# The passage from the z products into the SSD: a hand order on three engines, z's PSUM buffers swapped, two chunks prepared between z tiles

## The chip, the cores and the metric

One core of one Trainium2 chip. The metric is the device time of one execution, in microseconds (us). The engines are TensorE (PE, with PEld for its weight loads), VectorE (DVE), ScalarE (ACT), GpSimd (POOL) and SyncE (SP, which issues DMAs).

## The reference

One layer of an encoder over 1024 positions of width 1024: adaptive normalisation, one input projection, a Mamba-2 SSD group beside a chunked attention group, an output projection, then a gated convolutional FFN and a last normalisation. The part that matters here:

```
z, xbc, dt_raw, q, k, v = split(h @ w_in)
dt    = softplus(dt_raw + dt_bias);   A = -exp(a_log)
y     = ssd_scan(xs * dt, dt * A, bm, cm) + d_skip * xs      # per chunk, state carried on
y_ssd = rmsnorm(y * silu(z), norm_w)
x     = x + g_m * (concat[y_ssd, y_att] @ w_out)
```

In the kernel an SSD chunk has 128 positions (8 chunks). For each chunk: a decay mask per head `exp(seg) * (C B^T)` in two groups of 4 heads; `y_diag` (mask times `xdt = x * dt`); `y_off` (C times the state before); the new state (`xdd`, x with dt and the decay to the end, times B).

## The kernel before, in words

The program is a stream of instructions written in Python. A scheduler with its own timeline chooses the order on each engine, except where the code pins it: `tc.issue_after(i)` puts an instruction behind `i`, and the proxies `V`, `A`, `T` (class `InOrder`, for VectorE, ScalarE, TensorE) keep the written order while their `on` is true. In the SSD loop the helper `pe` chains TensorE's instructions in the order written. High-precision products are three matmuls of split operands (`mm3`, lines 76 to 78): high by high, high by low, low by high; `split` (lines 80 to 86) makes the high part on ScalarE and the low part on VectorE.

The stages around the change, in order:

- **z products.** h (`hH`, `hL`) times z's weights, in two column halves of 260 (`ch` 1, then 0), each in 8 tiles of 128 rows (`st` 0 to 7), 24 matmuls of 260 columns a tile. The weights of a half come in four parts (`wz_weights`): loaded into `raws`, split into `wzh` on ScalarE and `wzl` on VectorE. A tile lands in PSUM, either in a buffer of pool `psv` (tags `acc` and `pv`, named `zps`) or in one of two `s` buffers, and is emptied by a tanh on ScalarE (`zt`, line 628) and a multiply on VectorE (`zs`, line 629).
- **dt.** `dt_prep`: softplus of the 8 dt columns (`sm_...`), `adt`, its split `adh`/`adl`, sums over the chunk by three matmuls, and their exponentials (`ex`).
- **W_out.** Eight slots, loaded into `wos` or `raws` by `wout_get`, four of them scaled by a gate row (`wout_fold`), split by `wout_split` into the space of h (`hH`, `hL`) that z no longer needs. Slots 0 to 3 multiply the attention part, 4 to 7 the SSD part.
- **Preparing a chunk** (`ssd_pre`): `xdt` on VectorE, `xdd` on GpSimd, for each group the matrix `rm` (ScalarE and VectorE), its product `sg`, the products and transposes `cb`, and the mask `th` = exp(sg) * cb.
- **SSD loop**, chunk c: `ssd_y` (products `ydp`, `yop`, `stp`; then y, its gate with `zs`, its normalisation), `ssd_turn` of the chunk before (four transposes into `xps`, copied to `xs`), `ssd_pre` of chunk c + 1, and the output projection `wout_half(c)` (`wops`, 24 matmuls, whose right operand `yhl` is the split of attention or SSD output).

[...] While z runs, `acc` and `pv` are banks 0 and 1, the two `s` buffers banks 2-3 and 4-5, `tp` 6 and 7. In the SSD loop `xps` has 0 and 1, `wops` 2 and 3, and 4 to 7 go to `ydp`, `yop`, `stp`, `sg`; chunk 0's `ydp` is bank 4. In z's second half tile 7 has bank 4 before the change.

Of the kernel before, what the change touches and what calls it, by code (L numbers as in the profile page):

```python
# [40 lines left out]
def f32(ap):  # L41
    return ap.bitcast(F32)
# [22 lines left out]
def tile_block(ctx: ExitStack, tc: tile.TileContext, x, crep, pk, w_ada, w_first, w_ft, w_z,  # L65
# [14 lines left out]
    def split(hi, lo, src, ehi, elo, scale=None):  # L80
        if scale is not None:
            A.activation(hi, src, AF.Copy, scale=scale)
            V.scalar_tensor_tensor(lo, src, scale, f32(hi), op0=ALU.mult, op1=ALU.subtract)
            return
        i = A.activation(hi, src, AF.Copy) if ehi is A else ehi.tensor_copy(hi, src)  # L85
        return i, elo.tensor_tensor(lo, src, f32(hi), ALU.subtract)  # L86
# [501 lines left out]
    def wout_split(slot, t):  # L588
        dh, j = WORDER[slot]
        h, l = (n[slot // 4][:, slot % 4].rearrange("p a b -> p (a b)") for n in (hth, htl))  # L590
        with tc.issue_after(pin[0]), tc.issue_after(pin[1]):
            if j < 2:
                split(h, l, t, A, V)
            else:
                for b in range(2):
                    c = slice(512 * b, 512 * b + 512)
                    k = SNW + order[2 * j + b]
                    split(h[:, c], l[:, c], t[:, c], A, V, scale=pkt[:, k:k + 1])
        ws[dh] += [(h[:, k:k + 512], l[:, k:k + 512]) for k in (0, 512)]

    def rm512():
# [12 lines left out]
            ws.append((th_, tl_))  # L614
        return ws

    def z_tile(ch, st, wz):
        if st % 4 < 2:
            ps = psv.tile([P, 512], F32, tag=("acc", "pv")[st % 4], bufs=1, name="zps")[:, 0:260]
        else:  # L620
            ps = s_tile()[:, 0:260]
        for kt in range(KT):
            mm3(ps, hth[st // 4][:, st % 4, kt, :], htl[st // 4][:, st % 4, kt, :],
                wz[kt // 2][0][:, kt % 2, :],
                wz[kt // 2][1][:, kt % 2, :], kt == 0, kt == KT - 1)
# [3 lines left out]
        V.scalar_tensor_tensor(zs[:, st, ch * 260:ch * 260 + nz], th[:, 0:nz], 1.0, ps[:, 0:nz],
                               op0=ALU.add, op1=ALU.mult)  # L630
        if ch == 1:
            V.scalar_tensor_tensor(zs[:, st, 512:520], ps[:, 252:260], 2.0,
                                   pkt[:, DTB:DTB + 8], op0=ALU.mult, op1=ALU.add)

    def dt_prep():
# [13 lines left out]
        V.scalar_tensor_tensor(sm["p"], sm["p"], 1.0, sm["t"], op0=ALU.add, op1=ALU.mult)  # L649
        V.tensor_scalar(c8(sm["t"]), dtr, 0.0, None, op0=ALU.max)  # L650
        V.scalar_tensor_tensor(sm["dt"], sm["p"], 2.0, sm["t"], op0=ALU.mult, op1=ALU.add)
        V.scalar_tensor_tensor(sm["adt"].rearrange("p (c h) -> p c h", c=8),
                               sm["dt"].rearrange("p (c h) -> p c h", c=8), -1.0,
                               na.unsqueeze(1).to_broadcast([P, 8, 8]), op0=ALU.mult, op1=ALU.mult)
        pin[:] = [i.ins for i in split(adh, adl, sm["adt"], A, V)]
# [13 lines left out]
    def pe(op, *a, **k):  # L669
        with tc.issue_after(chain[0]) if chain and chain[0] else ExitStack():  # L670
            i = op(*a, **k)  # L671
# [3 lines left out]
    def ssd_pre(c, xp_, sgp_, between=None):
        cs = slice(c * P, (c + 1) * P)
# [3 lines left out]
        G.tensor_tensor(h8(xdd), h8(xdt), hb("de", c), ALU.mult)  # L680
        ms_ = []
        for g in range(2):
            rm = bcp.tile([P, 2, 4, P], F32R, tag="rm", bufs=2, name="rm")
            hs = slice(c * 8 + 4 * g, c * 8 + 4 * g + 4)
            for h in range(4):
                A.activation(rm[:, 0, h, :], tle, AF.Copy, scale=f32(adh)[:, hs.start + h:hs.start + h + 1])
            if g == 0:
                V.tensor_tensor(rm[:, 1], tle.unsqueeze(1).to_broadcast([P, 4, P]),
                                f32(adl)[:, hs].unsqueeze(2).to_broadcast([P, 4, P]), ALU.mult)
            else:  # L690
                for h in range(4):
                    A.activation(rm[:, 1, h, :], tle, AF.Copy,
                                 scale=f32(adl)[:, hs.start + h:hs.start + h + 1])
            sg = sgp_()
            for i in range(2):
                pe(T.matmul, sg, sgtr, rm[:, i].rearrange("p h l -> p (h l)"), start=i == 0, stop=i == 1)
            if g == 0:
                cbp = xp_()
                for i in range(2):
                    pe(T.matmul, cbp[:, i * P:(i + 1) * P], bt_[i][:, cs], ct_[i][:, cs],  # L700
                       start=True, stop=True)
                for i in range(2):
                    pe(T.transpose, cbp[:, (2 + i) * P:(3 + i) * P], bt_[i][:, cs], ident)
                cb = bcp.tile([P, 4, P], F32, tag="cb", bufs=1, name="cb")
                V.tensor_tensor(cb.rearrange("p (a b) l -> p a b l", a=2),
                                cbp.rearrange("p (a b l) -> p a b l", a=2, b=2),
                                tle1.unsqueeze(2).to_broadcast([P, 2, 2, P]), ALU.mult)
# [30 lines left out]
            wout_fold(wt[j])  # L738
    wz = wz_weights(0)
    wout_get(5, 2)  # L740
    for st in range(NT):
        z_tile(0, st, wz)
        if st == 0:
            wout_fold(wt[5])
            dt_prep()
        if st == 3:
            for j in (0, 1, 2):
                wout_split(j, wt[j])
            wout_get(3, 6, 7)
# [734 lines left out]
```

## Time and profile before

| what | us |
|---|---|
| median of 3 runs | 1232.65 (1231.15 to 1232.92) |
| profiled execution: span from first to last instruction | 1234.8 |
| profiled execution: its own time outside the span | not given by the page |
| TensorE (PE) busy | 1169.8 (95%) |
| VectorE (DVE) busy | 944.7 (77%) |
| ScalarE (ACT) busy | 589.0 (48%) |
| GpSimd (POOL) busy | 199.9 (16%) |
| z's second half, from its first product | 408.18 in the span |
| chunk 0's first product | 440.15 |
| chunk 1's first product | 453.12 |

Times in the lists below count from the first instruction. A timeline row has the start, the duration, engine, line of the code, operation, output and inputs, shapes, how many such instructions in a row, and in brackets the idle time of the engine before it with what ended it. In a row of waits the three numbers are the sum, how often, and the longest. The granted clock is the share of TensorE's full clock. A matmul of plain fp32 shows as two records.

### The profile page before, as it was taken

The page shows a single profiled execution, that of the slowest core. Times are in us where ns is not written, and L with a number is a line of the kernel's source. Part 1 is how long each engine was busy: PE and PEld are TensorE (multiplying, and loading weights), DVE is VectorE, ACT ScalarE, POOL GpSimd, SP SyncE. Part 2 cuts the span into 40 slices and gives each one's busy share as a digit, 9 for nine tenths or more (in the row PEclk, how much of TensorE's full clock was granted, in tenths as well). Part 3 has the DMA queues.
Part 4 walks back from the last instruction along what each step waited for, and adds up shares of the span by engine and source line. Part 5 has one row for each costly group of instructions (what it writes and reads, how often), then busy time and mean ns, then how long its engine had stood idle before and what let it go on. Part 6 is the DMA issues. An engine that isn't in the chain of part 4 may idle for free.

```text
span 1234.8 us, 15648 instructions
## 1 busy us (share of the span) xinstructions
PE 1169.8 (95%) x5802; PEld 983.1 (80%) x5802; DVE 944.7 (77%) x1419; ACT 589.0 (48%) x991; POOL 199.9 (16%) x174
## 2 busy tenths in 40 slices
PE   4998999989999969999999999999999999999995
PEld 3787788878878958888778888888888888888884
DVE  6836545589689667746799989888889869766976
ACT  4525555573333556666554434453434435433443
POOL 1304555575120033400000000000000000000002
PEclk9999999999999989999999999999999999999998
DMA  8712112134355301123132333222332277733533
GB/s 332 254 36 80 48 44 68 54 115 154 120 180 197 121 1 43 44 94 111 37 117 92 113 128 119 86 77 103 128 128 77 95 281 257 279 120 127 171 120 136
DMA packets 56395, 150.86 MB, mean 122 GB/s; under 512 B 5632, under 2 KB 5760, under 8 KB 54912
## 3 DMA queue, kind: packets, MB, share of 16 engines
q1 hardware_dynamic: 49264, 125.49, 29.8%
q10 hardware_dynamic: 7056, 24.38, 4.9%
q8 instruction: 45, 0.74, 0.2%
q14 instruction: 30, 0.25, 0.1%
HBM read 116.56 MB, written 29.10 MB: 118 GB/s over the span
## 4 chain that ended last, share of the span: by engine, by line
PE 80%; DVE 11%; ACT 3%; DMA 2%; issue 2%; POOL 1%; SPq 0%; DVEq 0%; POOLq 0%; ACTq 0%
PE wops L671 6%; PE dn L77 6%; PE dn L76 6%; PE dn L78 6%; PE uY L76 5%; PE uY L78 5%; PE uY L77 5%; PE uZ L78 3%; PE uZ L76 3%; PE uZ L77 3%; PE uX L76 3%; PE uX L78 3%; PE uX L77 3%; PE acc L76 2%; PE acc L77 2%; PE acc L78 2%
## 5 line engine op out<-in xcount | busy, mean ns | idle before, releaser
L903 POOL TENSOR_TENSOR st<-st,mhalf 128x1 f32<-128x1 f32 x16 | 12.7, 798 | 691.9 <-DVE st L902 680.5
L76 PE MATMUL dn<-w 128*128 128x512 f32 x308 | 111.9, 389 | 0.0
L77 PE MATMUL dn<-w 128*128 128x512 f32 x308 | 111.9, 389 | 0.0
L395 POOL TENSOR_SCALAR p<-p,st 128x640 f32<-128x640 f32 (+4 forms) x64 | 99.0, 1561 | 26.8 <-DVE st L394 23.7
L78 PE MATMUL dn<-w 128*128 128x512 f32 x308 | 103.3, 389 | 0.0
L76 PE MATMUL uY<-tH,w 128*128 128x512 f32 x256 | 99.7, 389 | 1.8 <-ACT w L58 1.8
L77 PE MATMUL uY<-tL,w 128*128 128x512 f32 x256 | 99.6, 389 | 0.0
L78 PE MATMUL uY<-tH,w 128*128 128x512 f32 x256 | 99.6, 389 | 0.0
L85 ACT ACTIVATE w<-ya 128x1024 fp32r<-128x1024 f32 (+1 forms) x41 | 39.1, 954 | 85.0 <-PE uY L78 82.7
L671 PE MATMUL wops<-hH,yhl 128*128 128x512 f32 x224 | 74.8, 402 | 3.5 <-DVE yhl L86 2.1
L76 PEld LDWEIGHTS dn<-w 128*128 128x128 f32 x308 | 57.8, 188 | 12.1
L77 PEld LDWEIGHTS dn<-w 128*128 128x128 f32 x308 | 57.8, 188 | 12.0
L78 PEld LDWEIGHTS dn<-w 128*128 128x128 f32 x308 | 57.8, 188 | 11.9
L389 DVE CUSTOM_DVE_ANT_0 p<-s,bias 128x640 f32<-128x640 f32 (+4 forms) x64 | 40.7, 650 | 26.3 <-PE tp L421 8.7
L76 PEld LDWEIGHTS uY<-tH,w 128*128 128x128 f32 x256 | 48.0, 188 | 12.0 <-ACT w L58 2.2
L78 PEld LDWEIGHTS uY<-tH,w 128*128 128x128 f32 x256 | 48.1, 188 | 10.0
L77 PEld LDWEIGHTS uY<-tL,w 128*128 128x128 f32 x256 | 48.0, 188 | 10.0
L86 DVE TENSOR_TENSOR pt<-tp,pt 128x512 fp32r<-128x512 f32 (+2 forms) x72 | 41.6, 595 | 18.4 <-ACT pt L85 11.4
L85 ACT ACTIVATE w<-xs 128x1024 fp32r<-128x1024 f32 (+1 forms) x41 | 38.9, 952 | 32.3 <-PE uY L78 32.3
L671 PEld LDWEIGHTS wops<-hH,yhl 128*128 128x128 f32 x224 | 42.4, 190 | 12.9 <-DVE yhl L86 2.5
L76 PE MATMUL s<-hH,wh 128*128 128x512 f32 x128 | 50.5, 395 | 1.5 <-DVE ct L492 1.3
L1054 DVE SCALAR_TENSOR_TENSOR a<-cv,pkt,a 128x1023 f32<-128x1023 f32 (+1 forms) x40 | 51.2, 1279 | 0.1
(444 smaller groups left out, 3428.8 us busy)
## 6 DMA issues: line engine op xcount, KB each, us to landing
gz<-a ACTq DMA_DIRECT2D x10, 1024.0 KB, 5.3
wos<-in_w_ada_dram SPq DMA_DIRECT2D x18, 512.0 KB, 4.1
ya<-in_w_up_dram SPq DMA_DIRECT2D x11, 768.0 KB, 4.1
xs<-in_w_up_dram SPq DMA_DIRECT2D x11, 768.0 KB, 4.2
adat<-in_w_ada_dram SPq DMA_DIRECT2D x16, 512.0 KB, 5.7
raws<-in_w_ft_dram SPq DMA_DIRECT2D x14, 512.0 KB, 3.5
qk<-in_w_ada_dram SPq DMA_DIRECT2D x14, 512.0 KB, 4.7
gy<-a ACTq DMA_DIRECT2D x10, 512.0 KB, 2.6
```

Of the source, the lines that this page charges most:

```text
L76: T.matmul(ps, lh, rh, start=start, stop=False, skip_group_check=more)
L77: T.matmul(ps, lh, rl, start=False, stop=False, skip_group_check=more)
L78: T.matmul(ps, ll, rh, start=False, stop=stop, skip_group_check=more)
L85: i = A.activation(hi, src, AF.Copy) if ehi is A else ehi.tensor_copy(hi, src)
L86: return i, elo.tensor_tensor(lo, src, f32(hi), ALU.subtract)
L389: V.tensor_tensor_reduce(out=dst, in0=src, in1=bsl, scale=-1.0, scalar=3e38, op0=ALU.add, op1=ALU.min, accum_out=nm)
L395: G.tensor_scalar(pv_, pv_, rr, None, op0=ALU.mult)
L671: i = op(*a, **k)
L903: G.tensor_tensor(r, ms, mhalf[:, 0:1], ALU.pow)
L1054: V.scalar_tensor_tensor(a[:, j:S], c[:, 0:S - j], w[2 - j], a[:, j:S], op0=ALU.mult, op1=ALU.add)
```

## The change

It changes the stretch from z's second half (`ch` 0) to the first SSD chunks:

1. z tiles use the `s` buffers for `st` 0, 1, 4, 5 and `acc`/`pv` for 2, 3, 6, 7, in both halves (before, the other way round). In the second half tile 7 now has bank 1 and tile 5 bank 4.
2. From the first z tile of half 0 on, `V`, `A` and `T` are in order, as written; TensorE's order goes on into the SSD loop's chain, VectorE's and ScalarE's ends after chunk 0's `ssd_y`.
3. `z_tile`, `dt_prep` and `ssd_pre` are cut into parts, and the parts are written between the z tiles: `dt_prep` behind tile 0, the sums (`dt_sums`) behind tile 1, chunk 0's masks behind tiles 2 to 4, chunk 1's `rm`, `xdt` and `xdd` behind tile 5, W_out's splits in between and after.
4. `wout_split` has no `issue_after` pins any more.

```diff
     def wout_split(slot, t):
...
-        with tc.issue_after(pin[0]), tc.issue_after(pin[1]):
-            if j < 2:
-                split(h, l, t, A, V)
...
+        if j < 2:
+            split(h, l, t, A, V)
...
-    def z_tile(ch, st, wz):
-        if st % 4 < 2:
-            ps = psv.tile([P, 512], F32, tag=("acc", "pv")[st % 4], bufs=1, name="zps")[:, 0:260]
+    def z_mm(ch, st, wz):
+        if st % 4 > 1:
+            ps = psv.tile([P, 512], F32, tag=("acc", "pv")[st % 4 - 2], bufs=1, name="zps")[:, 0:260]
         else:
             ps = s_tile()[:, 0:260]
...
-    for st in range(NT):
-        z_tile(0, st, wz)
-        if st == 0:
-            wout_fold(wt[5])
-            dt_prep()
-        if st == 3:
-            for j in (0, 1, 2):
-                wout_split(j, wt[j])
-            wout_get(3, 6, 7)
-            pre0 = ssd_pre(0, tp_tile, tp_tile)
-            wout_split(3, wt[3])
-        if st >= 4:
-            wout_split(st, wt[st])
+    V.on = A.on = T.on = True
+    V.last = A.last = T.last = None
+    zp = z_mm(0, 0, wz)
+    dt_prep()
+    z_evac(0, 0, zp)
+    zp = z_mm(0, 1, wz)
+    r0 = pre_rm(0, 0)
+    dt_sums()
+    x0 = pre_x(0)
+    z_evac(0, 1, zp)
+    wout_split(0, wt[0])
+    zp = z_mm(0, 2, wz)
+    r1 = pre_rm(0, 1)
+    g0 = pre_sg(r0, tp_tile())
+    z_evac(0, 2, zp)
+    zp = z_mm(0, 3, wz)
+    cb = pre_cb(0, tp_tile())
+    m0 = pre_m(0, g0, cb)
+    wout_fold(wt[5])
+    wout_split(1, wt[1])
+    z_evac(0, 3, zp)
+    zp = z_mm(0, 4, wz)
+    g1 = pre_sg(r1, tp_tile())
+    wout_split(2, wt[2])
+    wout_get(3, 6, 7)
+    m1 = pre_m(1, g1, cb)
+    pre0 = *x0, cb, [m0, m1]
+    z_evac(0, 4, zp)
+    zp = z_mm(0, 5, wz)
+    pre1 = {g: pre_rm(1, g) for g in range(2)}
+    pre1["x"] = pre_x(1)
+    z_evac(0, 5, zp)
+    zp = z_mm(0, 6, wz)
+    wout_split(3, wt[3])
+    wout_split(4, wt[4])
+    z_evac(0, 6, zp)
+    zp = z_mm(0, 7, wz)
+    wout_split(5, wt[5])
+    z_evac(0, 7, zp)
+    for j in (6, 7):
+        wout_split(j, wt[j])
...
-    chain[:] = [None]
+    T.on = False
+    chain[:] = [T.last]
     for c in range(NT):
         y = ssd_y(c, *pre)
+        V.on = A.on = False
```

What stands on the engines, with buffer numbers. In the changed kernel an instruction of a proxy that is in order has the line of `InOrder.issue` (L58).

TensorE at the start of z's second half, before (`zps_3779` is tile 0, `zps_3833` tile 1, `s_3861` tile 2; `wzh_3755` and `wzl_3756` are the first part of the weights, `wzh_3760` the second):

```order
L76 MATMUL zps_3779<-wzh_3755,hH0_83 128x260
L76 MATMUL zps_3833<-wzh_3755,hH0_83 128x260
L76 MATMUL s_3861<-wzh_3755,hH0_83 128x260
L77 MATMUL zps_3779<-wzl_3756,hH0_83 128x260
L78 MATMUL zps_3779<-wzh_3755,hL0_85 128x260
```

and now (`s_3779` is tile 0; `wzh_3765` and `wzl_3766` are the third part):

```order
L58 MATMUL s_3779<-wzh_3760,hH0_83 128x260
L58 MATMUL s_3779<-wzl_3761,hH0_83 128x260
L58 MATMUL s_3779<-wzh_3760,hL0_85 128x260
L58 MATMUL s_3779<-wzh_3765,hH0_83 128x260
L58 MATMUL s_3779<-wzl_3766,hH0_83 128x260
```

Before, tiles take turns; now the 24 matmuls of tile 0 follow each other through all four parts, and tile 1's stand behind them.

VectorE at the end of z, before (`s_4033` is tile 6, `s_4065` tile 7, `hL` W_out's low parts, `ydp_4135` chunk 0's product):

```order
L86 TENSOR_TENSOR hL0_85<-wos_2874,hH0_83 128x1024
L83 SCALAR_TENSOR_TENSOR hL1_86<-wos_2874,pkt_66,hH1_84 128x512 x2
L83 SCALAR_TENSOR_TENSOR hL1_86<-raws_68,pkt_66,hH1_84 128x512 x2
L83 SCALAR_TENSOR_TENSOR hL1_86<-wos_2874,pkt_66,hH1_84 128x512
L629 SCALAR_TENSOR_TENSOR zs_2862<-zt_4058,s_4033 128x260
L83 SCALAR_TENSOR_TENSOR hL1_86<-wos_2874,pkt_66,hH1_84 128x512
L83 SCALAR_TENSOR_TENSOR hL1_86<-raws_68,pkt_66,hH1_84 128x512 x2
L629 SCALAR_TENSOR_TENSOR zs_2862<-zt_4090,s_4065 128x260
L804 TENSOR_TENSOR yy_4144<-ydp_4135,yy_4144 128x512
```

and now (`s_3995` is tile 5, in bank 4; `zps_4042` tile 6, `zps_4076` tile 7):

```order
L58 SCALAR_TENSOR_TENSOR zs_2862<-zt_4039,s_3995 128x260
L58 TENSOR_TENSOR hL0_85<-wos_2874,hH0_83 128x1024
L58 SCALAR_TENSOR_TENSOR hL1_86<-wos_2874,pkt_66,hH1_84 128x512 x2
L58 SCALAR_TENSOR_TENSOR zs_2862<-zt_4073,zps_4042 128x260
L58 SCALAR_TENSOR_TENSOR hL1_86<-raws_68,pkt_66,hH1_84 128x512 x2
L58 SCALAR_TENSOR_TENSOR zs_2862<-zt_4105,zps_4076 128x260
L685 TENSOR_TENSOR xdt_4260<-xs_2848,sm_dt_2867 128x512
L58 SCALAR_TENSOR_TENSOR hL1_86<-wos_2874,pkt_66,hH1_84 128x512 x2
L695 TENSOR_TENSOR rm_4264<-tle1_2871,adl_2869 128x512
L58 SCALAR_TENSOR_TENSOR hL1_86<-raws_68,pkt_66,hH1_84 128x512
```

The evacuation of bank 4 stands ahead of W_out's last five slots instead of behind all of them, and the last two slots (6 and 7) stand behind the last evacuation, mixed with chunk 2's `xdt` and `rm`.

ScalarE at the end of z and in chunk 0, now (`state1_4129` is the state after chunk 0, `th_4202` and `th_4208` chunk 1's masks, `yt_4165` the square of chunk 0's y):

```order
L58 ACTIVATE state1_4129<-stp_4166 128x512
L723 ACTIVATE th_4202<-sg_4176 128x512
L693 ACTIVATE rm_4264<-tle1_2871,adh_2868 128x128 x4
L723 ACTIVATE th_4208<-sg_4205 128x512
L693 ACTIVATE rm_4298<-tle1_2871,adh_2868 128x128 x4
L699 ACTIVATE rm_4298<-tle1_2871,adl_2869 128x128 x4
L58 ACTIVATE yt_4165,st1_72<-yy_4163 128x512
```

Before, the square stood right behind the state, ahead of chunk 1's masks and chunk 2's `rm`.

More of the change, by code (lines that the diff above doesn't have):

```diff
@@ L654, in dt_prep, with dt_sums @@
                                na.unsqueeze(1).to_broadcast([P, 8, 8]), op0=ALU.mult, op1=ALU.mult)
-        pin[:] = [i.ins for i in split(adh, adl, sm["adt"], A, V)]
+        split(adh, adl, sm["adt"], A, V)
+    def dt_sums():
         dps = tp_tile()
@@ L673, in pe, with pre_x @@
             chain[0] = i.ins
[L675 to L676 removed]
+    def pre_x(c):
         xdt = bcp.tile([P, 512], F32, tag="xdt", bufs=2, name="xdt")
@@ L680, in ssd_pre, with pre_rm @@
         G.tensor_tensor(h8(xdd), h8(xdt), hb("de", c), ALU.mult)
+        return xdt, xdd
+    def pre_rm(c, g):
+        rm = bcp.tile([P, 2, 4, P], F32R, tag="rm", bufs=2, name="rm")
+        hs = slice(c * 8 + 4 * g, c * 8 + 4 * g + 4)
+        for h in range(4):
+            A.activation(rm[:, 0, h, :], tle, AF.Copy, scale=f32(adh)[:, hs.start + h:hs.start + h + 1])
+        if g == 0:
+            V.tensor_tensor(rm[:, 1], tle.unsqueeze(1).to_broadcast([P, 4, P]),
+                            f32(adl)[:, hs].unsqueeze(2).to_broadcast([P, 4, P]), ALU.mult)
+        else:
+            for h in range(4):
+                A.activation(rm[:, 1, h, :], tle, AF.Copy,
+                             scale=f32(adl)[:, hs.start + h:hs.start + h + 1])
+        return rm
@@ new lines, in pre_sg, with pre_cb @@
+    def pre_sg(rm, sg):
+        for i in range(2):
+            pe(T.matmul, sg, sgtr, rm[:, i].rearrange("p h l -> p (h l)"), start=i == 0, stop=i == 1)
+        return sg
+    def pre_cb(c, cbp):
+        cs = slice(c * P, (c + 1) * P)
+        for i in range(2):
+            pe(T.matmul, cbp[:, i * P:(i + 1) * P], bt_[i][:, cs], ct_[i][:, cs],
+               start=True, stop=True)
+        for i in range(2):
+            pe(T.transpose, cbp[:, (2 + i) * P:(3 + i) * P], bt_[i][:, cs], ident)
+        cb = bcp.tile([P, 4, P], F32, tag="cb", bufs=1, name="cb")
+        V.tensor_tensor(cb.rearrange("p (a b) l -> p a b l", a=2),
+                        cbp.rearrange("p (a b l) -> p a b l", a=2, b=2),
+                        tle1.unsqueeze(2).to_broadcast([P, 2, 2, P]), ALU.mult)
+        return cb
@@ L681, in ssd_pre, with pre_m @@
+    def pre_m(g, sg, cb):
+        m = th512().rearrange("p (h l) -> p h l", h=4)
+        pin1 = A.activation(m, sg.rearrange("p (h l) -> p h l", h=4), AF.Exp)
+        pin2 = V.tensor_tensor(m, m, cb[:, g:g + 1, :].to_broadcast([P, 4, P]), ALU.mult)
+        pin[:] = [pin1.ins, pin2.ins]
+        return m
+    def ssd_pre(c, xp_, sgp_, between=None, early=None):
+        xdt, xdd = early["x"] if early else pre_x(c)
         ms_ = []
         for g in range(2):
-            rm = bcp.tile([P, 2, 4, P], F32R, tag="rm", bufs=2, name="rm")
@@ L684, in ssd_pre @@
-            hs = slice(c * 8 + 4 * g, c * 8 + 4 * g + 4)
-            for h in range(4):
-                A.activation(rm[:, 0, h, :], tle, AF.Copy, scale=f32(adh)[:, hs.start + h:hs.start + h + 1])
+            sg = pre_sg(early[g] if early else pre_rm(c, g), sgp_())
             if g == 0:
[L688 to L707, printed above, removed]
+                cb = pre_cb(c, xp_())
```

23 lines of the change are left out of this document (12 added, 11 removed).

## The prediction

> **What bounds it now.** I read the page first (shares and the chain), then the waits of TensorE, then a table of stages from z's second half to the third SSD chunk, then the timelines of the engines there.
>
> ```profile
> span 1234.8 us, 15648 instructions
> PE 80%; DVE 11%; ACT 3%; DMA 2%; issue 2%; POOL 1%; SPq 0%; DVEq 0%; POOLq 0%; ACTq 0%
> ```
>
> TensorE carries the end; where it waits, the kernel loses time one to one. In the list of waits the longest single one behind the start-up is
>
> ```profile
> PE ydp L671 <- DVE zs L629: 6.5, 1, 6.5
> ```
>
> The table by stage has span, then busy time (and instructions) of PE, PEld, DVE, ACT, POOL, then the granted clock, DMA share and GB/s. Its stretches are: z's second half (weights of columns 0 to 259), the wait, chunk 0, chunk 1, chunk 2.
>
> ```profile
> 408.18:433.67 25.49, 25.49 (x210) 25.09 (x208) 19.48 (x42) 16.14 (x39) 2.31 (x3) 1.00 0.39 125
> 433.67:440.15 6.48, 0.00 (x1) 0.00 (x1) 6.43 (x9) 5.40 (x15) 2.56 (x2) 0.71 0.00 0
> 440.15:453.12 12.97, 12.97 (x54) 11.32 (x55) 4.77 (x7) 6.38 (x18) 3.70 (x4) 0.75 0.00 0
> 453.12:469.83 16.71, 13.17 (x63) 10.71 (x62) 9.94 (x13) 8.29 (x23) 5.25 (x5) 0.90 0.05 17
> 469.83:480.84 11.01, 11.01 (x63) 9.62 (x62) 10.39 (x14) 5.54 (x14) 5.68 (x6) 1.00 0.06 24
> ```
>
> z itself runs without a gap. Then TensorE stands still for 6.48 us, and chunk 0 runs at a clock of 0.75. The chain over the wait:
>
> ```profile
> 432.56 4.21 DVE hL L83 x4
> ...
> 438.36 1.41 DVE hL L83 x2
> 439.76 0.34 DVE zs L629
> 440.15 3.67 PE ydp L671 x16
> ```
>
> VectorE splits W_out first and empties the last z tile (L629) last; chunk 0's first product `ydp` goes into the PSUM bank (4) which that tile held. So 6.48 us pay for the place of one 0.4 us instruction, and for that bank.
>
> The clock afterwards, in stretches cut where the clock changes (same columns):
>
> ```profile
> 436.42:439.83 3.41, 0.00 (x0) 0.00 (x0) 3.41 (x7) 2.65 (x6) 0.00 (x0) 0.50 0.00 0
> 443.24:446.66 3.42, 3.42 (x11) 2.87 (x11) 2.02 (x4) 0.98 (x2) 0.89 (x1) 0.50 0.00 0
> 456.90:460.31 3.41, 1.97 (x14) 1.43 (x11) 3.41 (x5) 3.04 (x8) 3.41 (x3) 1.00 0.00 0
> 460.31:463.72 3.41, 1.31 (x6) 0.92 (x6) 3.41 (x5) 1.04 (x4) 1.81 (x3) 1.00 0.00 0
> 463.72:467.14 3.42, 3.42 (x10) 2.65 (x9) 0.05 (x1) 1.82 (x5) 0.00 (x0) 0.50 0.00 0
> ```
>
> Half clock lasts from 436.42 to 446.66, three pieces of 3.41. Of that, 440.15 to 446.66 lies on matmuls: 6.51 / 2 = 3.25 us lost. A second piece (463.72) follows a stretch in which TensorE was busy for 1.31 of 3.41; a stretch with 1.97 cost nothing.
>
> **The wait goes: +6.48.** The last two z tiles now take the banks 0 and 1 (`zps`), and `ydp` needs bank 4, which tile 5 held. By the new order tile 5's `zs` stands two z tiles (5.8 us) ahead of the end; chunk 0's masks and `xdt` stand earlier still. Nothing else releases `ydp`, so I take the whole wait; bounds: 6.48, and 5.2 if chunk 0's `xps` (bank 0, tile 6) waits until VectorE is as late as it is now (440.1 against the 438.8 at which TensorE gets there).
>
> **z's first tile now waits alone: -2.1.** Before, the scheduler put matmuls of tiles 0 to 3 between each other while weights came. Now all 24 of tile 0 stand first, in order.
>
> ```profile
> 410.18 0.64 ACT L82 ACTIVATE wzh<-raws 128x520 fp32r<-128x520 f32 x1 [1.41 <-DMA raws<-in_w_z_dram]
> 411.19 0.64 ACT L82 ACTIVATE wzh<-raws 128x520 fp32r<-128x520 f32 x1 [0.23 <-DMA raws<-in_w_z_dram]
> 410.85 0.70 DVE L83 SCALAR_TENSOR_TENSOR wzl<-raws,wzh 128x520 fp32r<-128x520 f32 x1 [1.17 <-ACT wzh L82]
> 411.86 0.70 DVE L83 SCALAR_TENSOR_TENSOR wzl<-raws,wzh 128x520 fp32r<-128x520 f32 x1 [0.20 <-ACT wzh L82]
> 433.27 0.28 PE L77 MATMUL s<-wzl,hH 128*128 128x260 f32 x1
> 433.39 0.28 PE L78 MATMUL s<-wzh,hL 128*128 128x260 f32 x1
> ```
>
> A product takes a slot of 0.12. Twelve run from 408.18 to 409.62; the thirteenth needs the third high part (410.82: 1.2 waited), the next the third low part (411.55: 0.6), and the fourth low part comes at 412.56 (0.3). Sum 2.1; 1.8 if the tile starts a little later. These waits lie within 2.9 us, and a piece of 3.41 that holds them all is busy for 1.3, like the one at 460.31, which half clock followed. That would add 3.41 / 2 = 1.7 (upper bound 3.8), but the piece must begin within 0.5 us of the right place, so I leave it to the rivals.
>
> [...]
>
> The sums of `dt` stand behind tile 1. VectorE's steps now follow each other without the fold, the z evacuation and the wait in between:
>
> ```profile
> 415.37 0.23 DVE L649 SCALAR_TENSOR_TENSOR sm_p<-sm_p,sm_t 128x64 f32<-128x64 f32 x1
> 418.89 0.22 DVE L651 SCALAR_TENSOR_TENSOR sm_dt<-sm_p,sm_t 128x64 f32<-128x64 f32 x1
> 419.14 0.22 DVE L652 SCALAR_TENSOR_TENSOR sm_e<-sm_dt,na 128x64 f32<-128x64 f32 x1
> ```
>
> The first ends at 415.60; three of 0.22 (the maximum taken like the two shown) and three gaps of 0.03 give 416.3, and tile 1 ends at 416.1: -0.2. So z ends at 408.18 + 25.49 + 2.3 = 436.0, against 433.67.
>
> **In order on ScalarE and VectorE: 0.** Up to 440.15 VectorE has 25.9 us of work and ScalarE 21.5 (first two stage rows), and the order must not make TensorE wait for them. I add durations in the new order. TensorE: sums to 417.0, tile 2 to 419.9, `sg` 0.5, tile 3 to 423.2, `cb` 0.7, tile 4 to 426.8, `sg` 0.5, tile 5 to 430.1, tile 6 to 433.0, tile 7 to 436.0. VectorE: tile 0's `zs` at 417, tile 1's at 418.5, tile 2's at 422 (behind ScalarE's eight `rm` pieces); `cb` from 424.0, mask to 425.3, fold (about 1.2) and split 1 (1.2), then tile 3's `zs`, done at 428.0; split 2, mask, tile 4's `zs`, `rm`, `xdt` to 431.3; tile 5's `zs` at 432.2; splits 3 and 4; tile 6's `zs` done at 436.0; split 5, tile 7's `zs` about 439. What TensorE needs of that: tile 0's and 1's `s` buffers at 423.9 and 427.3, tile 2's `acc` at 430.1 and tile 3's `pv` at 433.0, chunk 0's bank 4 at 436.0, `xps`'s bank 0 at 438.8. The tightest are the last one (cover 2.8) and `pv`. For `pv` the cover is 4.9; past a cover the price is one to one. The hidden cost has a row:
>
> ```profile
> 432.47 1.41 DVE L83 SCALAR_TENSOR_TENSOR hL<-wos,pkt,hH 128x512 fp32r<-128x512 f32 x2
> 433.80 2.98 DVE L83 SCALAR_TENSOR_TENSOR hL<-raws,pkt,hH 128x512 fp32r<-128x512 f32 x2
> 433.64 2.59 POOL L786 TENSOR_TENSOR yy<-xs,pkt 128x512 f32<-128x512 f32 x2 [5.07 <-PE s L77]
> ```
>
> While POOL works, the same VectorE pair takes twice as long. That now falls at 436 to 439, on slot 5's split; then VectorE has slots 6 and 7, chunk 2's `xdt` and `rm`, `cb` and chunk 1's masks to do before chunk 1's `ydp` at 445.7. I get the masks at about 445.1 and 445.7, the second needed 0.9 later: 0, up to -1.
>
> Chunk 1's `rm` and `xdt` were already made before the wait, so preparing two chunks adds little by itself. The removed pins of W_out's splits free what the hand order then fixes. W_out's slots 6 and 7 are loaded later, behind splits 1 and 2, in SP's queue with nothing urgent behind them:
>
> ```profile
> wos<-in_w_out_dram SPq DMA_DIRECT2D x10, 256.0 KB, 4.3
> ```
>
> Issued by 428 and 429, landed by 434; split from 436.3: 0. `affn`, `bffn` and `na` move by 0.5 us in all, beside waiting engines: 0. z's first half with swapped banks: the scheduler puts tiles 2 and 3 ahead of tile 1, whose bank the convolution still reads: 0.
>
> **Chunk 0 at full clock: +3.25.** From chunk 2's 11.01 us, without `yop` (472.48 - 471.56) and the turn (473.70 - 473.34), chunk 0 needs 9.73:
>
> ```profile
> 471.56 1.08 PE L671 MATMUL yop<-state,ct 128*128 128x256 f32 x4
> 472.48 1.03 PE L671 MATMUL stp<-xdd,cb 128*128 128x256 f32 x4
> 473.34 0.60 PE L671 MATMUL xps<-ident,yy 128*128 128x128 f32 x4
> 473.70 0.70 PE L671 MATMUL sg<-rm,sgtr 128*128 128x512 f32 x2
> ```
>
> 436.0 + 9.7 = 445.7 for chunk 1, against 453.12.
>
> **Chunk 1: -0.1.** ScalarE's square of chunk 0's `y` now stands behind chunk 2's `rm`, and chunk 0 is shorter, so the turn of `y` waits:
>
> ```profile
> 446.17 0.62 ACT L810 ACTIVATE yt<-yy 128x512 f32<-128x512 f32 x1
> 449.60 0.72 ACT L812 ACTIVATE yy<-yy,st 128x512 f32<-128x512 f32 x1 [1.07 <-POOL st L117]
> 455.12 0.69 DVE L804 TENSOR_TENSOR yy<-ydp,yy 128x512 f32<-128x512 f32 x1 [3.59 <-PE ydp L671]
> 459.79 0.50 PE L671 MATMUL wops<-hH,yhl 128*128 128x512 f32 x1 [1.44 <-ACT yhl L85]
> 462.62 0.73 PE L671 MATMUL wops<-hH,yhl 128*128 128x512 f32 x2 [2.10 <-DVE yhl L86]
> ```
>
> From square to scaled `y` 4.15 here, of which 1.5 is POOL's queue; I put the new wait at 1. But VectorE's run from `ydp` to the second `yhl` (455.12 to 462.6, 7.5) sets when the projection goes on, and what is waited earlier is not waited later: 3.54 becomes about 3.7. The half-clock piece stays.
>
> **Sum.** 6.48 - 2.1 - 0.2 + 3.25 - 0.1 = 7.3; 1234.8 - 7.3 = 1227.5. The page gives no time around the span, and the profiled execution lies 2.15 above the median 1232.65 (1231.15 to 1232.92). If the pieces lie otherwise against the program, one less of them falls on chunk 0, and the clock term is (6.51 - 3.41) / 2 = 1.55: the gain is then 5.6, which from the median gives 1227.0; with all 7.3 it would be 1225.4. I take 1227.0, which lies by the profiled sum too.
>
> **Rivals.** First, half clock follows tile 0's waits as worked out above, and chunk 1 could likewise get a second such piece, since its waits shift against the pieces. Price 1.7 each: 1228.7, with both 1230.4. For it speaks the row at 460.31; against it the stretch at 456.90, which with 1.97 busy cost nothing, and the narrow place.
>
> Second, the fixed order eats the gain: if VectorE slips by 9 us (4.9 cover, then 4 of waiting), tile 7 starts late: 1231, no change to be told. For it speaks the doubled pair above; against it that POOL has two 1 us instructions before 436.
>
> Third, slower: tile 0 waits for the load of its weights with no other tile to fill in. Each us by which that load is later costs one; the gain of 5.7 is spent when the last part lands at 416.9 and not 411.19, and with 8.7 us of delay the time is 1235.7.
>
> ```profile
> DMA to landing us min/median/max: 2.5/2.7/2.8
> ```
>
> Against it: these loads took 2.5 to 2.8 us.
>
> **Chances.** As summed 0.66 (1224.3 to 1228.2), clock 0.22 (1228.2 to 1230.4), order eats it 0.09, slower 0.03. About 0.2% (2.5 us) is what a measurement of this kernel can tell from no change. Faster 0.87, same 0.10, slower 0.03; range 1224.4 to 1230.2.
>
> **What would show it.** Between 409.6 and 412.6 three waits of tile 0 for `wzh` and `wzl`; no gap between z's last product and `ydp` at about 436; clock 1.00 from 436 to 446; chunk 1's `ydp` near 445.7; a wait of about 1 for the turn. It is wrong if TensorE waits between z tiles for a `zs`, if `xps` waits for tile 6, if chunk 1's masks are late by over 1 us, or if half clock follows tile 0.

## The result, and the profile after

The changed kernel took 1225.56 us (median; 1223.57 to 1227.74), the kernel before, on the same chip, 1232.49: a ratio of 0.9934 with a 95% interval of 0.9919 to 0.9948. In a second set (e5 below) it was 1226.18 and 0.9942 (0.9925 to 0.9960). So it is faster by 0.6 to 0.7%, some 7 to 8 us. The forecast of 1227.0 had the direction and the terms, but one term too small: it gave a gain of 5.65 by the medians, a ratio of 0.9954, where the medians measured 6.93 and 7.67. By the ratio the time is 1224.4 beside a before of 1232.49, the lower end of the forecast's range. One of e2's twelve runs below took 2998.64 and is left out.

The head of the page and of the chain, after:

```profile
span 1221.9 us, 15650 instructions
PE 79%; DVE 11%; ACT 3%; DMA 3%; issue 2%; POOL 1%; SPq 0%; DVEq 0%; POOLq 0%; ACTq 0%
```

TensorE still carries the end; it is busy for 1162.0 us where it was 1169.8. The timed run of this profiled execution took 1223.57, so 1.7 lies around the span. With the same 1.7, the profiled execution of before took about 1236.5, above every one of the four runs timed beside it.

The waits of TensorE from z's second half to chunk 2:

```profile
PE wops L678 <- ACT yhl L85: 1.4, 1, 1.4
PE xps L678 <- ACT yy L58: 1.2, 1, 1.2
PE wops L678 <- DVE yhl L86: 1.1, 1, 1.1
PE s L58 <- ACT wzh L82: 1.1, 1, 1.1
PE ydp L678 <- DVE th L724: 0.4, 1, 0.4
PE s L58 <- DVE wzl L83: 0.3, 1, 0.3
```

`ydp`'s 6.5 for `zs` is gone. New are the waits of z's tile 0 (1.1 and 0.3), the turn's (1.2) and that for chunk 1's mask (0.4). The stages, in the same columns as the table of before (z's second half, chunks 0, 1 and 2):

```profile
404.73:432.59 27.86, 26.37 (x211) 25.37 (x210) 19.97 (x43) 18.65 (x48) 2.09 (x2) 1.00 0.36 115
432.59:442.91 10.32, 9.89 (x56) 8.29 (x55) 10.32 (x15) 8.09 (x21) 5.36 (x4) 1.00 0.00 0
442.91:458.56 15.65, 11.90 (x62) 9.60 (x63) 11.97 (x18) 9.29 (x24) 5.93 (x7) 1.00 0.05 18
458.56:469.57 11.01, 11.01 (x63) 9.62 (x62) 10.39 (x14) 5.87 (x16) 5.68 (x6) 1.00 0.06 24
```

From z's first product to chunk 3 it is 64.84, where before it was 72.66: 7.82 less. The spans differ by 12.9, of which 3.45 lies ahead of z's second half. That does not look like the change's: z's first half takes 28.2 in both, and what lies ahead of it ended at 379.98 before and at 376.54 here, but at 377.58 in e6 (the same code as before up to there) and at 377.63 in e5 (the change). The granted clock is 1.00 in all four stages. But VectorE is busy for all 10.32 of chunk 0. Later work is not changed, and takes 1.63 less, about half of 3.41 (before had a half-clock piece at 603.67 that this execution lacks).

### The profile page after: what moved, and what is told of

The parts are those of the page before. It is cut to its first block, busy times and chain, and to the rows that moved or that the text cites. A ratio compares the mean times of both kernels' runs of the same rounds, so it can differ in the third digit from the quotient of the medians.

```text
span 1221.9 us, 15650 instructions
## 1 busy us (share of the span) xinstructions
PE 1162.0 (95%) x5802; PEld 976.2 (80%) x5802; DVE 945.9 (77%) x1419; ACT 589.1 (48%) x991; POOL 198.6 (16%) x174
## 4 chain that ended last, share of the span: by engine, by line
PE 79%; DVE 11%; ACT 3%; DMA 3%; issue 2%; POOL 1%; SPq 0%; DVEq 0%; POOLq 0%; ACTq 0%
PE dn L76 6%; PE dn L77 6%; PE dn L78 6%; PE wops L678 5%; PE uY L76 5%; PE uY L78 5%; PE uY L77 5%; PE uZ L78 3%; PE uZ L77 3%; PE uZ L76 3%; PE uX L78 3%; PE uX L77 3%; PE uX L76 3%; PE acc L76 2%; PE acc L77 2%
## 5 line engine op out<-in xcount | busy, mean ns | idle before, releaser
L85 ACT ACTIVATE pt<-tp 128x512 fp32r<-128x512 f32 (+2 forms) x72 | 36.2, 524 | 31.0 <-PE tp L421 14.1
```

## The experiments

All are timed against the kernel before on the same chip. The passage is counted from the first product of z's second half to chunk 3's `ydp`, in one profiled execution; a piece is a stretch of 3.41 at half clock. The pieces of an execution lie on a grid of 3.41 (in before they begin at 436.42, 439.83, 443.24, 463.72 and 603.67, whole multiples of 3.413 apart), and the stretches shown below are cut on that grid. The profiled execution is one of the timed runs and can lie far from the median: the change's (1223.57) is the shortest of its four, those of e3 (1232.11), e6 (1230.98) and e9 (1238.19) are the longest of their nine, five and twelve.

| kernel | median us | ratio, 95% | `ydp` of chunks 0, 1, 3 | pieces in the passage |
|---|---|---|---|---|
| before | 1232.4 to 1233.9 | | 32.0, 44.9, 72.7 | 4 |
| the change | 1225.6 | 0.9919 to 0.9948 | 27.9, 38.2, 64.8 | 0 |
| e5, again | 1226.2 | 0.9925 to 0.9960 | 29.1, 39.4, 67.5 | 2 |
| e1, banks alone | 1228.3 | 0.9947 to 0.9971 | 25.3, 37.1, 66.5 | 1 |
| e2, order alone | 1233.3 | 0.9989 to 1.0013 | 32.5, 45.4, 73.1 | 4 |
| e3, woven | 1228.1 | 0.9953 to 0.9981 | 25.3, 37.9, 69.6 | 4 |
| e4, TensorE's order alone | 1233.2 | 0.9992 to 1.0016 | 35.4, 45.1, 72.9 | 4 |
| e6, before kept busy | 1229.2 | 0.9953 to 0.9978 | 32.0, 41.8, 69.5 | 1 |
| e9, the same, small | 1231.6 | 0.9983 to 1.0010 | 32.0, 45.1, 73.5 | 4 |
| e7, change with 13 | 1227.5 | 0.9933 to 0.9963 | 29.1, 39.4, 66.7 | 1 |
| e8, woven, masks first | 1223.3 | 0.9908 to 0.9932 | 25.3, 35.1, 63.2 | 1 |
| e10, e8 kept busy | 1220.1 | 0.9888 to 0.9924 | 25.3, 35.1, 61.5 | 0 |
| e11, e1 kept busy | 1227.5 | 0.9924 to 0.9965 | 25.3, 37.1, 66.5 | 1 |
| e12, change with 5 | 1226.5 | 0.9923 to 0.9957 | 28.9, 39.3, 65.9 | 1 |

### e1 and e2: the banks without the order, the order without the banks

e1 is the kernel before with this edit, e2 the changed kernel with its reverse:

```diff
-        if st % 4 < 2:
-            ps = psv.tile([P, 512], F32, tag=("acc", "pv")[st % 4], bufs=1, name="zps")[:, 0:260]
+        if st % 4 > 1:
+            ps = psv.tile([P, 512], F32, tag=("acc", "pv")[st % 4 - 2], bufs=1, name="zps")[:, 0:260]
```

> The kernel before, with one edit: z's tiles 0, 1, 4, 5 of each half use the s buffers and 2, 3, 6, 7 the banks acc and pv. No hand order, no chunk prepared earlier. Theory A (the bank): ydp's wait for zs and the half clock behind it were all of the gain, so this kernel has nearly all of it. By row durations added in its order, from z's second half's first product: ydp at 25.2 (before 32.0, after 27.9), without a wait for zs; chunk 1's ydp at 36.6 (before 44.9, after 38.2), with a turn that waits 1.7 for tile 6's zs and about 1.5 for chunk 1's masks; chunk 2's at 52.6 (before 61.7, after 53.8). Time 1224 to 1227. Theory B (the hand order): VectorE, which splits W_out ahead of the last zs, only moves the wait from ydp to the turn and the masks; chunk 1's ydp at 42 or later, time 1229 or more.

> The changed kernel with z's banks as before (tiles 0, 1, 4, 5 in acc and pv, tiles 2, 3, 6, 7 in the s buffers); hand order and both prepared chunks stay. Theory A (the bank): ydp needs bank 4, which tile 7 holds, and waits about 3.5 for its zs, which stands behind split 5 on VectorE: from z's start ydp at 31 (after 27.9), chunk 1's at 41 (38.2). Time 1229, up to 1232 where half clock follows the wait (one to two pieces of 3.41 on matmuls, 1.7 each). Theory B (the order): tile 7's zs comes in time, the wait is under 1, time 1226.

e1's waits of TensorE in the passage:

```profile
PE wops L671 <- DVE yhl L86: 2.1, 1, 2.1
PE xps L671 <- DVE zs L629: 1.8, 1, 1.8
PE wops L671 <- ACT yhl L85: 1.4, 1, 1.4
PE ydp L671 <- DVE th L712: 1.4, 1, 1.4
```

and e2's longest:

```profile
PE ydp L678 <- DVE zs L58: 3.4, 1, 3.4
```

Theory A holds for the wait. With the banks alone `ydp` waits for nothing; 1.8 and 1.4 of the late VectorE come back at `xps` (bank 0, which tile 6 held) and at chunk 1's mask, where 1.7 and 1.5 were expected. With the order alone `ydp` waits 3.4 for a `zs`, four half-clock pieces fall into the passage, chunk 0 takes 12.9 where it took 10.3 in the change, and nothing is gained at all (1.0001). e1's median, 1228.3, lies between theory A's 1227 and theory B's 1229. A piece falls into chunk 1 of its profiled execution, which would explain the difference; no run shows that it does so in the timed runs. The stretch ahead of it and the piece:

```profile
454.44:457.85 3.41, 1.31 (x6) 0.92 (x6) 3.41 (x5) 1.04 (x4) 1.82 (x3) 1.00 0.00 0
457.85:461.27 3.42, 3.42 (x10) 2.68 (x9) 0.05 (x1) 1.81 (x5) 0.00 (x0) 0.50 0.00 0
```

That is the row at 460.31 of before, almost digit by digit. e2 missed its upper end of 1232 by 1.3; in its profiled execution half clock came behind tile 0's waits too (1.97 busy, then 0.50):

```profile
404.21:407.62 3.41, 1.97 (x13) 1.50 (x12) 2.17 (x6) 1.48 (x4) 0.00 (x0) 1.00 0.36 111
407.62:411.03 3.41, 3.41 (x18) 3.41 (x17) 2.86 (x13) 0.05 (x1) 0.00 (x0) 0.50 0.88 287
```

### e4: TensorE's order alone

```diff
-    V.on = A.on = T.on = True
-    V.last = A.last = T.last = None
+    T.on = True
+    T.last = None
```

> The changed kernel with the hand order on TensorE alone; VectorE and ScalarE in the scheduler's order. Theory A (the bank is all that counts): ydp still waits for no zs, time 1225 to 1227. Rival (TensorE's written order needs the others' written order): the sums of dt, which now have a fixed place behind tile 1, wait about 4.3 for VectorE, which does other work first; ydp at 31 from z's start (after 27.9), chunk 1's at 41.4, time 1228.5 to 1230.5, with another 1.7 where half clock follows that wait.

```profile
PE tp L58 <- DVE sm_e L657: 3.8, 1, 3.8
```

The rival holds: the sums of `dt` have a fixed place and wait 3.8 for VectorE, which does W_out's splits and a fold in between. Two pieces follow that wait (from 417.91 and 421.33, behind a stretch busy for 1.51 of 3.41) and one follows tile 0, `ydp` comes at 35.4 where the rival had 31, and the time is that of before, 1 above what the rival allowed with half clock (1232.2). No product waits for a `zs` here either. So a written order on TensorE alone cost what the bank gave.

### e5: the change again

The same kernel, unchanged.

> The changed kernel itself, once more, beside the others of this call. [...] Median 1225.6 again, single runs 1223.5 to 1229 with the mean clock falling from 0.992 to 0.988 as the time rises. If the passage itself varies (waits, transfers), the time would vary at one and the same mean clock.

The six runs went from 1222.22 (mean clock 0.993) to 1229.37 (0.986). Its profiled execution, at 1228.80, has two pieces in the passage. Tile 0's stretch and what follows, chunk 1's stretch and what follows:

```profile
407.25:410.66 3.41, 1.91 (x12) 1.31 (x10) 2.00 (x5) 1.52 (x4) 0.00 (x0) 1.00 0.38 124
410.66:414.08 3.42, 3.42 (x18) 3.42 (x17) 2.93 (x14) 0.00 (x0) 0.00 (x0) 0.50 0.78 265
451.62:455.03 3.41, 1.13 (x6) 0.46 (x4) 3.41 (x4) 3.20 (x9) 2.02 (x3) 1.00 0.00 0
455.03:458.45 3.42, 3.13 (x7) 2.48 (x8) 1.44 (x3) 0.72 (x1) 1.19 (x2) 0.50 0.00 0
```

The same stretches in the first execution, where neither piece came (tile 0's, the next, two of chunk 1):

```profile
406.50:409.92 3.42, 2.12 (x13) 1.71 (x14) 2.23 (x6) 1.52 (x4) 0.00 (x0) 1.00 0.35 118
409.92:413.33 3.41, 3.38 (x28) 3.17 (x28) 2.65 (x13) 0.34 (x2) 0.00 (x0) 1.00 0.74 246
447.47:450.88 3.41, 1.78 (x12) 1.46 (x12) 3.01 (x4) 2.66 (x7) 2.81 (x3) 1.00 0.00 0
450.88:454.29 3.41, 2.07 (x8) 1.41 (x9) 3.23 (x5) 1.89 (x6) 1.58 (x3) 1.00 0.00 0
```

The waits are the same to 0.2 in both; only where the stretches of 3.41 begin differs, by 0.35 against z's first product (1.77 and 1.42). So what differs between these two passages, by 2.66, is the clock and not the work.

### e6 and e9: the wait kept busy

The kernel before, with 26 matmuls that nobody reads ahead of chunk 0's first product (z's last tile is kept in the written order on TensorE besides, so that they stand behind it); e9 has 64 columns of plain fp32 in place of 512. e6's edit:

```diff
+    def warm(n, ps=None):
+        ps = x_tile() if ps is None else ps
+        for _ in range(n):
+            pe(T.matmul, ps, sgtr, ws[0][0][0], start=True, stop=True)
...
-    chain[:] = [None]
+    chain[:] = [T.last]
+    warm(26)
```

> The kernel before, with 26 matmuls (128x512, about 0.23 each, 6.0 in all) written into a free bank that nobody reads, between z's last product and chunk 0's ydp: TensorE is busy while it would wait for zs. The wait itself stays. Theory (half clock follows a stretch of 3.41 in which TensorE is busy for less than about half): ydp at 32 from z's second half's first product as before, then no half clock: chunk 0 takes 9.7 instead of 12.97, and the time falls by 3.25 to 1229.4 (1231.1 if one of the pieces falls elsewhere in the runs that are timed). Rival (chunk 0's 12.97 was VectorE's or ScalarE's late work, and the clock a by-product): chunk 0 stays over 12, 1232.7.

> As e6 (the kernel before, 26 unread matmuls in the wait for zs), but plain fp32 matmuls of 128x64, like ydp's own, in place of 128x512 ones. Eight of ydp's take 1.89, so 26 fill the wait as long as before (6.1), with an eighth of the columns. Theory (what counts is the time in which TensorE is at work): the same as e6, chunk 0 in 9.8, 1229.2, mean clock 0.990. Rival (what counts is what streams through it, columns or array rows): half clock follows in spite of them, chunk 0 in 12 to 13, 1232.7 or more, mean clock 0.985. It also tells whether chunk 0's own ydp (sixteen records of 64 columns) holds the clock down once it is down.

e6, the wait and chunk 0:

```profile
431.28:437.76 6.48, 5.95 (x26) 4.53 (x25) 6.43 (x9) 5.41 (x15) 2.56 (x2) 1.00 0.00 0
437.76:447.57 9.81, 9.81 (x54) 8.58 (x55) 5.38 (x7) 6.08 (x18) 4.00 (x4) 1.00 0.01 2
```

The wait is still 6.48 long, and chunk 0 takes 9.81, where 9.73 were forecast and 12.97 measured before. The median came to 1229.17 (forecast 1229.4). This is the clock term of the sum by itself: 0.34% (0.22 to 0.47%), about 4.2 us (2.7 to 5.8). That holds the 3.25 of the profiled execution and not the 1.55 that the forecast took.

e9 went to the rival: chunk 0 took 13.1 and nothing was gained (0.9997), though its median lies 1.1 below the rival's 1232.7. Its small matmuls, and the stretches, in the longest of its runs:

```profile
434.35 5.92 PE L671 MATMUL xps<-xs,ident 128*128 128x64 f32 x52
```

```profile
434.54:437.95 3.41, 3.41 (x33) 3.41 (x32) 3.41 (x4) 3.41 (x11) 2.52 (x2) 1.00 0.00 0
437.95:441.37 3.42, 2.69 (x25) 2.56 (x24) 2.98 (x6) 1.96 (x5) 0.00 (x0) 1.00 0.00 0
441.37:444.78 3.41, 3.41 (x17) 3.32 (x17) 0.33 (x1) 0.00 (x0) 0.00 (x0) 0.50 0.02 5
444.78:448.20 3.42, 3.42 (x13) 2.96 (x12) 2.40 (x4) 2.01 (x6) 1.91 (x2) 0.50 0.00 0
```

The stretch that is full of them (3.41) is not followed by half clock, the one with 2.69 of 3.41 is; stretches of chunks 0 to 2 that were busy for 1.97 (before), 2.07 (the change), 2.15 and 2.93 (e10) and 2.24 (e12) at full clock were not followed by it. e6's 26 matmuls show as 26 records and e9's as 52, so the columns and the number format change together, and which of the two counts stays open. And the stretch from 441.37, full of chunk 0's own `ydp` at half clock, is followed by another piece, as the one from 439.83 in before is, busy for 3.09; why, no run shows. e9's 12 runs spread over 1228.8 to 1238.2, e6's five over 1228.8 to 1231.0.

### e3 and e8: z's first tiles woven, then the masks first

e3 writes tiles 0 to 2 by weight part:

```diff
+        for k0 in (0, 4, 6):
+            for st, ps in zip(sts, pss):
+                for kt in range(k0, 4 if k0 == 0 else k0 + 2):
+                    mm3(ps, ...
```

> The changed kernel with z's tiles 0, 1 and 2 of the second half written together: the products of the first two weight parts for the three tiles, then those of the third, then of the fourth. Chunk 0's first sg stands behind tile 3. Theory A (each us that TensorE waits is lost): the waits of tile 0 for wzh and wzl (2.1 by the forecast, 1.75 measured) go, ydp comes at 25.2 from z's start (after 27.9) and the time falls by 1.2 to 2, to 1223.6 to 1224.4: not all, since chunk 1's masks come no earlier and chunk 1's ydp then waits 2 for them. Rival (VectorE sets the end of this passage): ydp comes earlier, but chunk 1's ydp waits for th by as much as was gained, 1225.6 as the change.

`ydp` came at 25.3 as expected; the rest missed, 1228.1 where 1223.6 to 1225.6 were expected. Chunk 1's `ydp` waited 2.7 for `th`, which VectorE made behind W_out's last splits (the first pair here took 2.65, while GpSimd worked, and not 1.41), and the stretch of that wait was busy for 1.05. VectorE's rows and GpSimd's, then the stretch and the one behind it:

```profile
438.60 2.65 DVE L58 SCALAR_TENSOR_TENSOR hL<-wos,pkt,hH 128x512 fp32r<-128x512 f32 x2
441.17 1.40 DVE L58 SCALAR_TENSOR_TENSOR hL<-raws,pkt,hH 128x512 fp32r<-128x512 f32 x2
...
445.12 0.68 DVE L739 TENSOR_TENSOR th<-th,cb 128x512 f32<-128x512 f32 x1
439.20 1.49 POOL L865 TENSOR_TENSOR state<-state,ex 128x512 f32<-128x512 f32 x1
```

```profile
442.29:445.70 3.41, 1.05 (x8) 0.97 (x8) 3.41 (x9) 0.41 (x1) 0.00 (x0) 1.00 0.00 0
445.70:449.12 3.42, 3.32 (x13) 3.00 (x13) 1.29 (x3) 2.39 (x8) 0.81 (x2) 0.50 0.02 5
```

Four pieces fell into chunk 1 of this execution, which took 20.7. So the rival holds: VectorE sets the end, and chunk 1's `ydp` came at 37.9, only 0.3 ahead of the change's. That half clock made the timed runs dearer than the rival said is argued from this one execution, the longest of nine. e8 therefore puts chunk 1's masks ahead of what nobody waits for yet, and moves half of chunk 2's first `rm` from VectorE to ScalarE:

```diff
-    for j in (6, 7):
-        wout_split(j, wt[j])
...
+        m0 = pre_m(0, g0, cb)
+        wout_split(6, wt[6])
+        copy()
+        g1 = pre_sg(pre1[1], sg_tile())
+        m1 = pre_m(1, g1, cb)
...
+        if c == 0:
+            wout_split(7, wt[7])
```

> The woven first tiles of e3, and VectorE's and ScalarE's hand order carried on to chunk 1's masks: these stand ahead of W_out's last two splits and of chunk 0's y, and the second half of chunk 2's first rm is made on ScalarE. Theory (chunk 1 of e3 was late because VectorE made its masks behind work that nobody waited for yet): ydp at 25.2 from z's start, chunk 1's ydp at 35 (e3 37.9, the change 38.2), no wait for th, a wait of 1.3 for the turn; chunk 3's ydp at 61.7 (e3 69.6, the change 64.8) if no half clock falls into it; time 1222.5 to 1224.5, below the change by 1.1 to 3. Rival (VectorE is full, and what is put behind the masks comes back as a longer wait for yhl): chunk 3's ydp at 64.8, 1225.6.

Chunk 1's `ydp` came at 35.1 and the time fell to 1223.26, as expected. The ratio is clear of e3's and of e1's, but its interval overlaps the change's. The wait for `th` did not vanish, it fell from 2.7 to 0.5 (e10's row, the same 0.5 as in e8):

```profile
PE ydp L693 <- DVE th L58: 0.5, 1, 0.5
```

### e7, e10, e11, e12: chunk 1 kept busy

Five unread matmuls ahead of chunk 1's first `wops` (e7 has four ahead of the turn and four ahead of the product that waits for VectorE's `yhl` besides):

```diff
+            if n == 1 and dh == 0 and k == 0:
+                warm(5)
```

> The changed kernel with 13 unread matmuls of 128x512 in chunk 1's three waits of TensorE: 4 ahead of the turn, 5 ahead of the first wops, 4 ahead of the product that waits for VectorE's yhl. Theory: no stretch of chunk 1 is then busy for less than half, no half clock from z's end to chunk 3 in any execution: the mean clock of the timed runs rises by 0.0014 for each piece that the change had there. By row durations the added matmuls delay chunk 2 by up to 0.6. Time 1224.5 to 1226.2. Rival (the added matmuls take bank or weight-load time from the real ones): slower than the change by 1 or more, at the same clock.

> The kernel of e8 with five unread matmuls of 128x512 (1.15 in all) ahead of chunk 1's first wops, in a wait of 1.42 for ScalarE's yhl. In e8's profile that wait lies in a stretch of 3.41 that is busy for 1.79, and a half-clock piece of 1.7 follows. Theory: the piece goes, nothing is delayed: chunk 3's ydp at 61.5 from z's start (e8 63.15), time 1221.6 (e8 1223.26), mean clock up by 0.0014. Rival (the piece was there in few of the timed runs, or comes one stretch later): 1223.3, no difference.

> The kernel of e1 (banks alone) with five unread matmuls of 128x512 (1.15) ahead of chunk 1's first wops, in the wait of 1.4 for ScalarE's yhl. Theory (in the passage the hand order is worth nothing of its own; e1 differed from the change by half-clock pieces alone): the piece of e1 in chunk 1 goes, chunk 3's ydp at 64.7 from z's start (e1 66.45, the change 64.84 without a piece and 67.50 with two), time 1225.5 to 1227, as the change or a little less. Rival (the order itself is worth the difference of e1 and the change, 2 to 3): 1228.3, as e1.

> The changed kernel with the same five unread matmuls ahead of chunk 1's first wops (not the 13 of e7). Theory: no delay, no piece in chunk 1; the piece behind z's tile 0 stays in those executions that have it. Chunk 3's ydp at 64.8 from z's start, 66.5 with a piece behind tile 0; time 1224.5 to 1226, equal to e11 within 1.5. Rival (the pieces of chunk 1 cost the timed runs nothing): 1226.2 as the change.

On e8 it worked in the profiled execution: passage 61.5 as expected, no piece. The timed runs point the same way, 0.9906 against the 0.9920 of e8 (1.7 us), and a mean clock of 0.990 to 0.993 against 0.987 to 0.990, but the intervals of the ratios overlap. The median, 1220.09, is 1.5 below the expected one, and so is that of the kernel before in its set (1232.38 against 1233.85). e8's stretch ahead of its piece:

```profile
447.48:450.89 3.41, 1.79 (x7) 1.16 (x7) 3.41 (x5) 2.83 (x9) 3.41 (x3) 1.00 0.00 0
```

and e10's:

```profile
446.80:450.21 3.41, 2.93 (x13) 1.76 (x12) 3.41 (x5) 2.80 (x8) 3.41 (x3) 1.00 0.00 0
```

On the other three it bought nothing that can be told. e7 and e12 kept the piece behind tile 0, which the filling does not touch; e7 missed its 1224.5 to 1226.2 by 1.3, e12 its 1224.5 to 1226 by 0.5. e7's 13 also delayed chunk 1, which took 16.27 where it took 15.65 in the change without a piece. e11 (0.5 above its 1227) filled the wrong wait: its stretch of 1.33 lies on VectorE's `yhl` (2.1 of waiting), not on ScalarE's:

```profile
451.36:454.78 3.42, 1.33 (x6) 1.05 (x6) 3.33 (x5) 1.06 (x4) 1.69 (x3) 1.00 0.00 0
454.78:458.19 3.41, 3.41 (x9) 2.64 (x9) 0.10 (x1) 1.88 (x6) 0.00 (x0) 0.50 0.00 0
```

So whether the hand order is worth anything beside the banks stays open: e1 and e11 (1228.3, 1227.5) lie 1 to 3 above the change and e12 (1225.6 to 1226.5), but the intervals of their ratios overlap. The woven and longer order of e8 did pay beside the banks: 0.9920 (0.9908 to 0.9932) against e1's 0.9959 (0.9947 to 0.9971).

## Where the prediction held, and the step that failed

**The wait goes (+6.48): right.** No product waits for a `zs` any more, and the cause is the bank: e1 removes it with one line, e2 brings 3.4 of it back.

**Tile 0 alone (-2.1), the sums (-0.2): right.** z's second half took 27.86 against 25.49, 2.37 more where 2.3 were forecast. The products that waited:

```profile
406.06 0.28 PE L58 MATMUL s<-wzh,hL 128*128 128x260 f32 x1
407.44 0.39 PE L58 MATMUL s<-wzh,hH 128*128 128x260 f32 x1 [1.10 <-ACT wzh L82]
408.17 0.39 PE L58 MATMUL s<-wzl,hH 128*128 128x260 f32 x1 [0.35 <-DVE wzl L83]
```

The brackets count from the end of a record of 0.28. From start to start, less a slot of 0.12, the three waits are 1.26, 0.61 and 0.18 (the third at 409.18), where 1.2, 0.6 and 0.3 were worked out; the sums came 0.19 late.

**VectorE and ScalarE in order (0, up to -1): right.** No z tile waits; chunk 1's mask is 0.4 late. That VectorE is the next limit e3 showed: 2.7 of waiting as soon as TensorE came earlier.

**Chunk 0 at full clock (+3.25): right, and then cut down wrongly. This is the step that failed.** In the profile chunk 0 took 10.32, with the 0.4 of the mask, at clock 1.00. To reach the medians, the forecast supposed that in the timed runs one piece less falls on chunk 0, and took 1.55 in place of 3.25. e6 measured the term in timed runs: 0.22 to 0.47%, or 2.7 to 5.8 us. Part at least of what made the profiled execution long lay elsewhere: z's second half begins at 408.18 in it and at 405.79 in e6. A wait of 6.48 leaves at least one stretch of 3.41 idle for 3.07 or more wherever the grid lies, and a half-clock piece that began on chunk 0's `ydp` or just ahead of it was followed by another in before (439.83, then 443.24) and in e9 (441.37, then 444.78). Nor does 1227.0 lie by the profiled sum: 1227.5 is a span, and with the 1.7 around it the time is 1229.2.

With the uncut sum of 7.3 the median of before gives 1225.4, and the measured ones are 1225.56 and 1226.18. That they lie so close is in part luck: the sum holds neither the piece behind tile 0 (1.1 to 1.3 where it came) nor the 1.06 that chunk 1 gained in the first execution by losing its piece.

**Chunk 1 (-0.1): the waits right, the piece not as said.** The waits for `yhl` and the turn are 3.7, as forecast. "The half-clock piece stays" held in e5's execution (17.05) and not in the first, where chunk 1 took 15.65 and not 16.71. It is neither kept nor gone: between the two executions the waits were the same to 0.2, and the begin of the stretches of 3.41 differed by 0.35.

**The first rival, half clock behind tile 0, had too small a chance (0.22), as far as four executions tell.** The piece came in three of the four profiled executions with the change's order there (e5, e7, e12; not the first), and in e2 and e4. The forecast asked for a stretch busy for 1.3; stretches of 1.91 (e5), 1.95 (e7), 1.97 (e2) and 2.04 (e12) were followed by a piece, the one of 2.12 (the first execution) was not. The longest gap of tile 0 was 1.0 in e5, where half clock followed, and 1.1 in the first execution, where it did not. Its price was 1.1 to 1.3 (27.9 to 28.9 and 29.1) where 1.7 was put: of z's products 28 pass in a stretch at full clock (the first execution's row at 409.92) and 18 at half (e5's at 410.66), and ten of 0.12 are 1.2. With both pieces the rival's time was put at 1230.4; the execution that had both took 1228.80. The four timed runs look like a mixture of it and of the forecast's case: two have a mean clock of 0.992 and two of 0.989.

## What to carry to other kernels

Ask of each wait of the engine that carries the end which buffer it waits for, and not only who is late: one line that moves a bank away from the last evacuation was worth about 5 (3.6 to 6.5) of the 7 to 8 us here, and the written order without it was worth nothing. Then read the granted clock behind the waits that remain, and how long TensorE was busy in the stretch ahead of each half-clock piece. In this kernel such a piece came, in and just ahead of chunks 0 and 1, behind stretches of 3.41 that were busy for 0.67 (before, from 433.00) to 1.79 (e8), with e9's small products for 2.69; where one shows, either remove the wait or try to fill it with matmuls that nobody reads. In the wait of 6.48, 26 of 512 columns were worth 0.34%; in chunk 1's short waits the timed runs could not tell a gain. And where the executions of a kernel differ by whole pieces of clock, take the size of a term from several executions or from an experiment, not from one profile cut down by a guess.

## What the runs showed of the hardware

- The half-clock pieces lie on a grid of 3.413 us: in before, half clock begins at 64.37, 112.15, 129.22, 248.68, 436.42, 463.72 and 603.67, which are 14, 5, 35, 55, 8 and 41 such steps apart, in the first execution of the change at 61.76, 109.55 and 246.08 (14 and 40 steps). Against z's first product the grid lay at 0.93 in before, 1.42 in e5, 1.59 in e10 and 1.77 in the first execution; what sets it no run shows. A shift of 0.35 went with two pieces more (e5 against the first execution). Over 32 runs the kernel before went from 1230.6 at a mean clock of 0.987 to 1237.7 at 0.981.
- The time in which TensorE was busy does not by itself tell where half clock came. In and just ahead of chunk 1, stretches busy for 1.05 (e3), 1.13 (e5), 1.31 (before, e1), 1.33 (e11) and 1.79 (e8) of 3.41 were followed by half clock, and those of 1.78 and 2.07 (the change), 1.97 (before), 2.24 (e12) and 2.93 (e10) were not. Among z's products of 260 columns a stretch of 2.04 (e12) was followed by it and one of 2.12 (the change) was not; with e9's 64-column fp32 products one of 2.69 was.
- e10's five unread matmuls cost nothing that shows: the wait of chunk 1's first `wops` for ScalarE's `yhl` fell from 1.4 (e8) to 0.3, that `wops` came 43.98 after z's first product with and without them, and chunk 1 took 15.4. e7's 13 made chunk 1 0.6 longer (16.27 and 15.65).
